# Products on ones, a 128-row spread of the norm weights and a fixed order in the opening of a two-layer trunk

## The chip, the core and the metric

The kernel runs on one core of one Trainium2 chip. The metric is the device time of one execution in microseconds (us), lower is better. Engines are TensorE (PE, its weight loads PEld), VectorE (DVE), ScalarE (ACT), GpSimd (POOL) and SyncE (SP), whose queue issues most loads.

## The reference

x has 512 tokens of 1024 features. Layer 0 has mixer A, layer 1 mixer B (latent attention); each layer ends with a squared-ReLU MLP. What matters here is the beginning of mixer A:

```python
h = rms_norm(x, attn_norm[0])
proj = h @ w_in                      # 1024 x 2120
q, k, v, qi, ki, wi = jnp.split(proj, cuts, axis=-1)
qi = partial_rope(qi.reshape(bsz, seq, IDX_HEADS, IDX_DIM), cos_i, sin_i, IDX_ROT)
ki = partial_rope(ki[:, :, None, :], cos_i, sin_i, IDX_ROT)[:, :, 0, :]
logits = jnp.einsum('bthd,bsd->bths', qib, ki)
score = jnp.einsum('bths,bth->bts', jax.nn.relu(logits), wib)
_, sel = lax.top_k(score, top_k)     # 128 of at most 512 keys for each token
```

Columns 1536 to 2120 of `w_in` (qi, ki, wi) feed the selection; the other 1536 columns are q, k and v.

## The kernel before

**Tiles.** Four token tiles of 128 rows, `xt[0..3]`. Tile 0 is special: its queries may see 128 keys at most, so no selection is needed, and only its 64 `ki` columns are computed. The order of the tiles is therefore 1, 2, 3, 0.

**Products in three passes.** Every float32 operand is split into a high and a low part. `mm3` makes three products for each pair: high x high (L227), high x low weight (L228), low activations x high weight (L229).

**Weights.** The class `Weights` holds one list of chunks for the whole program. `fetch` loads the next chunk on SP's queue into one of three raw buffers (L109). `convert` makes `w_hi` (mostly ScalarE, L143) and `w_lo` = raw - `w_hi` (GpSimd, or VectorE where the chunk says "v"; L150) in one of five pairs of buffers. `take` hands chunks to the consumer and converts some ahead. The columns 1536 to 1828 come in three chunks `w0`, `w1`, `w2` of 3, 3 and 2 blocks of 128 rows, the columns 1828 to 2120 in `w3`, `w4`, `w5`, the columns of k and v in `w6` and so on.

**Norm.** The row of norm weights is loaded into one partition (`g_row`), and two products with a row of ones (`one_row`, K = 1) spread it over 128 partitions in PSUM (`g_ps`, L316). `gains` multiplies a tile by it in two halves of 512 columns (`h`, VectorE, L477). `turn` transposes `h` with TensorE in two groups of four (`tps`, L454); ScalarE copies each group as `hT_hi` (L458), VectorE subtracts for `hT_lo` (L459). `factor` squares the tile (ScalarE, `junk`, L483), and a small VectorE operation (L484) and a GpSimd power (L485) make the factor 1/rms, which is applied when results leave PSUM (`out_of`, L715).

**The opening.** `idx_rows` multiplies tiles 1 to 3 with `w0` to `w2` (`ip`, 24 products of 292 columns for a tile); `rope_tables` makes the angles' sines and cosines on VectorE and ScalarE; `idx_tile` multiplies the four tiles with `w3` to `w5` (tile 0: 24 products of 64 columns). Then `proj_tiles` begins with the products of k and v (`pp`), among which the scores are computed. VectorE then runs the top-k selection beside the further projections.

**Order.** The tile framework orders the instructions of each engine by priorities and its own estimate of times. Only inside `with tc.manual_schedule(...)` does an engine keep the order of the code; before the change that holds for TensorE from `idx_tile` on. An engine works through its row strictly in order.

## Time and profile before

| | us |
|---|---|
| median of 3 runs (1151.34 to 1152.82) | 1151.39 |
| profiled execution | 1150.95 |
| its span, first to last instruction | 1149.2 |
| TensorE busy in the span | 1117.5 (97%) |
| VectorE / ScalarE / GpSimd busy | 754.8 / 619.7 / 670.0 |

Busy TensorE is the sum of overlapping, pipelined products, so 97% doesn't mean that it works at its peak. In a timeline a row gives start, length, engine, source line, output <- inputs and shape; the spacing of starts, not the length, is what a product costs in a dense row. Idle time in front of an instruction and what ended it stand in square brackets.

### The profile page before, as it was taken

How to read it: one execution, taken by the hardware profiler on the slowest of the kernel's cores; microseconds unless marked ns; L12 is line 12 of the kernel's file. 1: busy time of each engine (PE TensorE's matmuls, PEld its weight loads, DVE VectorE, ACT ScalarE, POOL GpSimd, SP SyncE). 2: the span in 40 equal slices, each digit the busy share in tenths (PEclk: the TensorE clock that was granted, in tenths of full speed). 3: DMA queues.
4: the chain of work that ended last, by engine and by line, in shares of the span. 5: the costliest groups of instructions: out<-in, count | busy, mean ns of one | idle time of the engine just before them, and what ended most of it. 6: DMA issues, size and time to landing. Idle time of an engine off the chain costs nothing.

```text
span 1149.2 us, 16018 instructions
## 1 busy us (share of the span) xinstructions
PE 1117.5 (97%) x5725; PEld 949.2 (83%) x5725; DVE 754.8 (66%) x1399; ACT 619.7 (54%) x1143; POOL 670.0 (58%) x508
## 2 busy tenths in 40 slices
PE   8999899989999999999999999899999999999997
PEld 7788788869888888888889898787988888888886
DVE  6699798673566466466566788676556466556664
ACT  6574896534544554454445776563564454464452
POOL 5498533543657857856702643554557756865772
PEclk9999999989999999999999999999999999999999
DMA  6413100242224314413322200111424313412402
GB/s 200 123 55 110 38 1 1 76 150 87 75 72 147 106 58 130 133 58 103 86 62 79 76 23 34 56 56 56 167 63 138 128 49 117 147 61 87 147 10 83
DMA packets 65465, 99.04 MB, mean 86 GB/s; under 512 B 3173, under 2 KB 41833, under 8 KB 65386
## 3 DMA queue, kind: packets, MB, share of 16 engines
q1 hardware_dynamic: 65386, 98.03, 26.9%
q8 instruction: 45, 0.74, 0.3%
q14 instruction: 34, 0.28, 0.1%
HBM read 95.92 MB, written 2.10 MB: 85 GB/s over the span
## 4 chain that ended last, share of the span: by engine, by line
PE 90%; DVE 3%; ACT 3%; issue 2%; POOL 1%; DMA 1%; SPq 0%; DVEq 0%; POOLq 0%; ACTq 0%
PE dn L1226 23%; PE up L227 10%; PE up L229 10%; PE up L228 10%; PE s_ps L560 3%; PE o_ps L622 3%; PE pt_ps L579 2%; PE wo_ps L227 2%; PE wo_ps L228 2%; PE wo_ps L229 2%; PE pp L227 2%; PE pp L229 2%; PE pp L228 2%; PE tps L454 1%; PE dn L228 1%
## 5 line engine op out<-in xcount | busy, mean ns | idle before, releaser
L148 POOL TENSOR_TENSOR w_lo<-quad,w_hi 128x512 fp32r<-128x512 f32 x196 | 274.7, 1433 | 163.1 <-ACT w_hi L143 155.7
L150 POOL TENSOR_TENSOR w_lo<-w_raw,w_hi 128x1024 fp32r<-128x1024 f32 (+4 forms) x117 | 264.4, 2278 | 86.7 <-ACT w_hi L143 71.6
L1229 DVE TENSOR_TENSOR x<-dn,x 128x512 f32<-128x512 f32 x196 | 134.9, 690 | 139.5 <-PE dn L1226 139.4
L228 PE MATMUL up<-hT_lo,w_hi 128*128 128x512 f32 (+1 forms) x576 | 210.8, 367 | 0.0
L227 PE MATMUL up<-hT_hi,w_hi 128*128 128x512 f32 (+1 forms) x576 | 210.3, 368 | 0.0
L229 PE MATMUL up<-hT_hi,w_lo 128*128 128x512 f32 (+1 forms) x576 | 208.8, 367 | 0.0
L143 ACT CAST w_hi<-w_raw 128x1024 fp32r<-128x1024 f32 (+6 forms) x112 | 111.7, 1006 | 141.1 <-PE dn L1226 62.2
L143 ACT CAST w_hi<-quad 128x1024 fp32r<-128x1024 f32 x98 | 101.2, 1050 | 100.0 <-DVE quad L86 71.7
L1226 PE MATMUL dn<-w_hi,lh 128*128 128x512 f32 x392 | 152.5, 389 | 0.0
L1226 PE MATMUL dn<-w_lo,lh 128*128 128x512 f32 x392 | 152.5, 389 | 0.0
L1226 PE MATMUL dn<-w_hi,ll 128*128 128x512 f32 x392 | 152.5, 389 | 0.0
L1191 DVE TENSOR_TENSOR ll<-u,lh 128x512 fp32r<-128x512 f32 x106 | 99.2, 966 | 40.7 <-ACT lh L1190 40.7
L229 PEld LDWEIGHTS up<-hT_hi,w_lo 128*128 128x128 f32 x576 | 109.1, 190 | 17.6
L227 PEld LDWEIGHTS up<-hT_hi,w_hi 128*128 128x128 f32 x576 | 109.0, 190 | 17.6 <-ACT hT_hi L458 0.2
L228 PEld LDWEIGHTS up<-hT_lo,w_hi 128*128 128x128 f32 x576 | 109.1, 190 | 17.4
L86 DVE TENSOR_TENSOR quad<-quad 128x1024 f32<-128x1024 f32 x56 | 68.4, 1221 | 65.3 <-POOL w_lo L148 65.3
L1190 ACT CAST lh<-u 128x512 fp32r<-128x512 f32 x106 | 62.9, 620 | 75.0 <-DVE u L1203 66.6
L1226 PEld LDWEIGHTS dn<-w_hi,ll 128*128 128x128 f32 x392 | 73.6, 188 | 15.3
L1226 PEld LDWEIGHTS dn<-w_hi,lh 128*128 128x128 f32 x392 | 73.6, 188 | 15.3
L1226 PEld LDWEIGHTS dn<-w_lo,lh 128*128 128x128 f32 x392 | 73.6, 188 | 15.3
L573 ACT ACTIVATE p<-p,m 128x128 f32<-128x128 f32 (+3 forms) x128 | 72.0, 564 | 16.3 <-DVE m L568 15.5
L592 ACT CAST pt_hi<-pt_ps 128x128 fp32r<-128x128 f32 (+3 forms) x128 | 53.0, 423 | 27.8 <-PE pt_ps L579 25.3
(237 smaller groups left out, 2249.8 us busy)
## 6 DMA issues: line engine op xcount, KB each, us to landing
w_raw<-in_mlp_w_up_dram SPq DMA_DIRECT2D x64, 512.0 KB, 3.7
quad<-in_mlp_w_down_dram SPq DMA_DIRECT2D x56, 512.0 KB, 3.6
w_raw<-in_a_w_in_dram SPq DMA_DIRECT2D x12, 512.0 KB, 3.6
w_raw<-in_a_w_out_dram SPq DMA_DIRECT2D x8, 512.0 KB, 3.2
w_raw<-in_mlp_w_down_dram SPq DMA_DIRECT2D x8, 512.0 KB, 4.5
w_raw<-in_b_w_out_dram SPq DMA_DIRECT2D x8, 512.0 KB, 3.7
x<-in_x_dram SPq DMA_DIRECT2D x4, 512.0 KB, 7.5
w_raw<-in_b_w_kv_up_dram SPq DMA_DIRECT2D x4, 512.0 KB, 3.9
```

The lines of the kernel that those rows point to most:

```text
L86: self.nc.vector.tensor_sub(q[o], q[l], q[r])
L143: nc.scalar.copy(h, v)
L148: nc.gpsimd.tensor_sub(l[:, cs], v[:, cs], h[:, cs].bitcast(F32))
L150: (nc.gpsimd if engs[1] == "p" else nc.vector).tensor_sub(l, v, h.bitcast(F32))
L227: nc.tensor.matmul(ps, lh, rh, start=first, stop=False)
L228: nc.tensor.matmul(ps, lh, rl, start=False, stop=False)
L229: nc.tensor.matmul(ps, ll, rh, start=False, stop=last)
L573: nc.scalar.activation(U["p"][:, :N], U["p"][:, :N], AF.Exp, bias=U["m"], scale=-1.0, accum_out=pair["sums"][:, c:c + 1])
L1190: nc.scalar.copy(lh, v)
L1191: nc.vector.tensor_sub(ll, v, lh.bitcast(F32))
L1226: nc.tensor.matmul(pp[t], l[:, k, ts], r[:, k, :], start=first and k == 0 and m == 0, stop=k == 1 and m == 2, skip_group_check=True)
L1229: last = nc.vector.tensor_add(x[:, cs], pp[t], x[:, cs])
```

## The change

1. Before any input has landed, seven products of a 128x128 tile of ones (kept in `xt[0]`) run on TensorE into the bank `rest`.
2. `g_row` becomes a tile of 128 rows of zeros, whose row 0 is loaded by ScalarE's queue; the spread uses the 128x128 matrix `first` (row 0 ones, others zero) in place of `one_row`.
3. The first chunk is split: `w0` has one block, `w1` two, `w2` three, `w3` two. So what was `w3` is now `w4`. Tile 1 is loaded in two halves, and the order on SP's queue is written out: tile 1, `w0`, `w1`, tile 2, `w2`, positions, tile 3, `w3`, tile 0.
4. The order of TensorE, ScalarE and VectorE in the opening is written by hand. The products of the fourth chunk with tile 1 stand ahead of the transposes of tile 0. `take(1, 4)` converts nothing ahead; `W.ahead(n)` does where it is called.
5. The square and the factor are separate (`squares`, `factor`); `rope_tables` stands behind the factor of tile 3.
6. `ang` and the first steps of `turns` are kept in PSUM instead of SBUF.

```diff
+    def ahead(self, n):
+        while len(self.done) < min(self.taken + n, len(self.items)):
+            self.convert()
...
-    W.rows(a_w_in[0][0:3 * P], 1536, 1828, 3, "av")
+    W.rows(a_w_in[0][0:P], 1536, 1828, 1)
+    W.rows(a_w_in[0][P:3 * P], 1536, 1828, 2, "av")
...
+    g_row = ht.tile([P, D], F32, name="g_row", tag="h", bufs=2)
+    first = const.tile([P, P], F32, name="first")
+    with tc.high_priority(2000):
+        nc.vector.memset(g_row[:, 0:512], 0.0)
+        nc.gpsimd.memset(g_row[:, 512:D], 0.0)
+        nc.scalar.dma_start(g_row[0:1], attn_norm[0:1])
+    nc.vector.memset(xt[0][:, 0:P], 1.0)
+    rest = bank("rest", 7)
+    for _ in range(7):
+        nc.tensor.matmul(rest[:, 0:P], xt[0][:, 0:P], xt[0][:, 0:P], start=True, stop=True)
+    nc.vector.memset(first, 0.0)
+    nc.vector.memset(first[0:1], 1.0)
...
-        nc.tensor.matmul(g_first[c], one_row, g_row[:, c * 512:(c + 1) * 512], start=True, stop=True)
+        nc.tensor.matmul(g_first[c], first, g_row[:, c * 512:(c + 1) * 512], start=True, stop=True)
...
-            ang = tp.tile([P, 2, NT, n], F32, name="ang")
+            both = bank("ang", 4)
+            ang, turns = (both[:, o:o + 2 * NT * n].rearrange("p (a t n) -> p a t n", a=2, t=NT) for o in (0, 256))
...
+                with tc.manual_schedule(engines={mybir.EngineType.PE, mybir.EngineType.Activation,
+                                                 mybir.EngineType.DVE}):
+                    nm.gains(1)
+                    w0, w1 = W.take(1, 4)[0], W.take(1, 4)[0]
+                    nm.turn(1)
+                    idx_rows(1, 0, w0)
+                    idx_rows(1, 1, w1)
+                    w2 = W.take(1, 4)[0]
+                    nm.gains(2)
+                    nm.turn(2)
+                    idx_rows(2, 0, w0)
+                    idx_rows(2, 1, w1)
+                    ps = token_positions(pr)
+                    w3 = W.take(1, 4)[0]
+                    nm.gains(3)
+                    idx_rows(1, 3, w2)
+                    nm.turn(3)
+                    nc.vector.tensor_copy(pos, ps[:, :NT])
+                    nm.squares(pr, 1)
+                    idx_rows(2, 3, w2)
+                    idx_rows(3, 0, w0)
+                    idx_rows(3, 1, w1)
+                    idx_rows(3, 3, w2)
+                    nm.gains(0)
+                    idx_rows(1, 6, w3)
+                    nm.turn(0)
+                    nm.squares(pr, 2)
+                    W.ahead(1)
+                    nm.squares(pr, 3)
+                    W.ahead(2)
+                    nm.factor(1)
+                    out_of(inat[1][:, :292], ips[1][:, :292], 1)
+                    nm.squares(pr, 0)
+                    W.ahead(3)
+                    idx_rows(2, 6, w3)
+                    nm.factor(2)
+                    idx_rows(3, 6, w3)
+                    nm.factor(3)
+                with tc.issue_after(nm.factored.ins):
+                    rope_tables()
```

Where the instructions stand now is shown at three places. Numbers behind names are buffer numbers; `tps` and `hT` of the rows belong to the tile that the text names.

ScalarE before, from the copy of tile 1's second half to the first of tile 3 (`tps_230`); `w3` and `w4` are the first two chunks of the columns 1828 to 2120.

```order
L458 CAST hT_hi_131<-tps_150 128x4x128
L143 CAST w2_hi_167<-w2_raw_97 128x584
L458 CAST hT_hi_131<-tps_185 128x4x128
L483 ACTIVATE junk_388,lead_71<-x0_84 128x1024
L143 CAST w3_hi_212<-w3_raw_100 128x876
L458 CAST hT_hi_131<-tps_192 128x4x128
L143 CAST w4_hi_361<-w4_raw_165 128x876
L458 CAST hT_hi_131<-tps_230 128x4x128
```

The changed kernel's ScalarE, from the chunk `w3` to the chunk `w5`; `tps_302` and `tps_309` are tile 0, `w4` is what `w3` was.

```order
L148 CAST w3_hi_231<-w3_raw_118 128x584
L482 CAST hT_hi_150<-tps_249 128x4x128
L482 CAST hT_hi_150<-tps_256 128x4x128
L505 ACTIVATE junk_264,lead_71<-x1_85 128x1024
L482 CAST hT_hi_150<-tps_302 128x4x128
L482 CAST hT_hi_150<-tps_309 128x4x128
L505 ACTIVATE junk_316,lead_71<-x2_86 128x1024
L148 CAST w4_hi_318<-w4_raw_121 128x876
L505 ACTIVATE junk_324,lead_71<-x3_87 128x1024
L148 CAST w5_hi_326<-w5_raw_199 128x876
```

The cast of that chunk moved from ahead of tile 3's copies to behind tile 0's copies and a square.

GpSimd before, from the second chunk's low half on.

```order
L150 TENSOR_TENSOR w1_lo_162<-w1_raw_94,w1_hi_161 128x876
L485 TENSOR_TENSOR lead_71<-lead_71,neghalf_69 128x1
L150 TENSOR_TENSOR w2_lo_168<-w2_raw_97,w2_hi_167 128x584
L485 TENSOR_TENSOR lead_71<-lead_71,neghalf_69 128x1 x2
L150 TENSOR_TENSOR w3_lo_213<-w3_raw_100,w3_hi_212 128x876
L150 TENSOR_TENSOR w4_lo_362<-w4_raw_165,w4_hi_361 128x876
```

GpSimd in the changed kernel; the rows on `lead` are the powers of the factors.

```order
L155 TENSOR_TENSOR w2_lo_196<-w2_raw_114,w2_hi_195 128x876
L155 TENSOR_TENSOR w3_lo_232<-w3_raw_118,w3_hi_231 128x584
L511 TENSOR_TENSOR lead_71<-lead_71,neghalf_69 128x1 x2
L155 TENSOR_TENSOR w4_lo_319<-w4_raw_121,w4_hi_318 128x876
L511 TENSOR_TENSOR lead_71<-lead_71,neghalf_69 128x1
L155 TENSOR_TENSOR w5_lo_327<-w5_raw_199,w5_hi_326 128x876
L511 TENSOR_TENSOR lead_71<-lead_71,neghalf_69 128x1
L155 TENSOR_TENSOR w6_lo_338<-w6_raw_235,w6_hi_337 128x584
```

Each of the low halves `w4`, `w5` and `w6` now has powers ahead of it, which wait for squares of ScalarE.

VectorE in the changed kernel, from tile 1's first gain half on; `h_161`, `h_201`, `h_237` are tiles 1, 2, 3.

```order
L501 TENSOR_TENSOR h_161<-x1_85,g_ps_124 128x512
L501 TENSOR_TENSOR h_161<-x1_85,g_ps_125 128x512
L155 TENSOR_TENSOR w1_lo_169<-w1_raw_111,w1_hi_168 128x584
L483 TENSOR_TENSOR hT_lo_151<-tps_172,hT_hi_150 128x4x128
L483 TENSOR_TENSOR hT_lo_151<-tps_179,hT_hi_150 128x4x128
L501 TENSOR_TENSOR h_201<-x2_86,g_ps_124 128x512
L501 TENSOR_TENSOR h_201<-x2_86,g_ps_125 128x512
L483 TENSOR_TENSOR hT_lo_151<-tps_204,hT_hi_150 128x4x128
L483 TENSOR_TENSOR hT_lo_151<-tps_211,hT_hi_150 128x4x128
L352 CAST posf_227<-posi_104 4x128
L501 TENSOR_TENSOR h_237<-x3_87,g_ps_124 128x512
```

VectorE in the kernel before, over the same work.

```order
L477 TENSOR_TENSOR h_182<-x2_86,g_ps_107 128x512
L484 TENSOR_SCALAR lead_71<-lead_71 128x1
L459 TENSOR_TENSOR hT_lo_132<-tps_143,hT_hi_131 128x4x128
L477 TENSOR_TENSOR h_227<-x3_87,g_ps_106 128x512
L477 TENSOR_TENSOR h_227<-x3_87,g_ps_107 128x512
L484 TENSOR_SCALAR lead_71<-lead_71 128x1
L459 TENSOR_TENSOR hT_lo_132<-tps_150,hT_hi_131 128x4x128
L340 CAST posf_320<-posi_102 4x128
```

The cast of the positions stood behind tile 3's gains and stands ahead of them now; the gains of tiles 2 and 3 stood ahead of `hT_lo` and stand behind it now.

## Rows read from the trace of the kernel before

**Rows 1.** The page, part 4: the chain that ended last, by engine.
```profile
PE 90%; DVE 3%; ACT 3%; issue 2%; POOL 1%; DMA 1%; SPq 0%; DVEq 0%; POOLq 0%; ACTq 0%
```

**Rows 2.** TensorE's waits over the span: total us, times, longest.
```profile
PE g_ps L316 <- DMA g_row<-in_attn_norm_dram: 4.3, 1, 4.3
```

**Rows 3.** Stages: length, busy us (count) by engine, granted clock, DMA share, GB/s.
```profile
60.00:117.00 57.00, 57.00 (x261) 46.76 (x261) 54.81 (x147) 33.06 (x62) 49.14 (x63) 1.00 0.28 85
...
130.00:180.00 50.00, 47.55 (x318) 41.12 (x316) 46.38 (x140) 45.02 (x132) 18.34 (x17) 1.00 0.00 1
```

**Rows 4.** Timeline of TensorE in the opening: start us, length us, what.
```profile
4.26 3.75 PE L316 MATMUL g_ps<-g_row,one_row 1*128 1x512 f32 x4 [4.26 <-DMA g_row<-in_attn_norm_dram]
...
10.72 0.61 PE L227 MATMUL ip<-w_hi,hT_hi 128*128 128x292 f32 x1 [0.52 <-ACT hT_hi L458]
...
14.06 0.45 PE L227 MATMUL ip<-w_hi,hT_hi 128*128 128x292 f32 x1
...
14.51 0.30 PE L229 MATMUL ip<-w_hi,hT_lo 128*128 128x292 f32 x1
14.64 0.29 PE L227 MATMUL ip<-w_hi,hT_hi 128*128 128x292 f32 x1
...
15.17 0.60 PE L454 MATMUL tps<-ident,h 128*128 128x128 f32 x4
15.53 0.38 PE L229 MATMUL ip<-w_hi,hT_lo 128*128 128x292 f32 x1
...
34.79 0.20 PE L227 MATMUL ip<-w_hi,hT_hi 128*128 128x64 f32 x1
...
37.39 0.48 PE L227 MATMUL pp<-w_hi,hT_hi 128*128 128x512 f32 x1
```

**Rows 5.** Timeline of SP's queue: the load of the norm weights.
```profile
1.17 0.33 SPq L306 DMA_DIRECT2D g_row<-in_attn_norm_dram  x1
```

**Rows 6.** Timeline of VectorE in the opening.
```profile
0.80 0.06 DVE L232 MEMSET ones<- 128x1 f32 x1 [0.80 <-PEq L1283]
...
6.34 0.69 DVE L477 TENSOR_TENSOR h<-x,g_ps 128x512 f32<-128x512 f32 x1 [0.55 <-PE g_ps L316]
7.36 1.07 DVE L150 TENSOR_TENSOR w_lo<-w_raw,w_hi 128x876 fp32r<-128x876 f32 x1 [0.33 <-ACT w_hi L143]
...
13.16 1.20 DVE L340 CAST posf<-posi 4x128 f32<-4x128 int32 x1
```

**Rows 7.** Timeline of ScalarE in the opening.
```profile
8.15 1.06 ACT L483 ACTIVATE junk<-x 128x1024 bf16<-128x1024 f32 x1 [0.82 <-DMA x<-in_x_dram]
...
9.26 0.92 ACT L143 CAST w_hi<-w_raw 128x876 fp32r<-128x876 f32 x1
10.09 0.58 ACT L458 CAST hT_hi<-tps 128x512 fp32r<-128x512 f32 x1
...
14.20 0.92 ACT L143 CAST w_hi<-w_raw 128x876 fp32r<-128x876 f32 x1
```

**Rows 8.** Timeline of GpSimd in the opening.
```profile
1.06 0.52 POOL L322 MEMSET smask<- 128x512 f32 x1
...
12.85 1.44 POOL L150 TENSOR_TENSOR w_lo<-w_raw,w_hi 128x584 fp32r<-128x584 f32 x1
14.24 0.55 POOL L485 TENSOR_TENSOR lead<-lead,neghalf 128x1 f32<-128x1 f32 x1
...
15.61 4.11 POOL L150 TENSOR_TENSOR w_lo<-w_raw,w_hi 128x876 fp32r<-128x876 f32 x2
```

**Rows 9.** The page, part 6: loads, KB each, median us from issue to landing.
```profile
x<-in_x_dram SPq DMA_DIRECT2D x4, 512.0 KB, 7.5
```

**Rows 10.** Stages of one us behind a gap of TensorE, columns as in rows 3.
```profile
250.00:251.00 1.00, 0.00 (x0) 0.00 (x0) 1.00 (x1) 0.58 (x1) 0.98 (x1) 0.50 1.06 377
...
256.00:257.00 1.00, 1.00 (x7) 1.00 (x7) 1.00 (x3) 0.00 (x0) 0.00 (x0) 0.60 1.04 385
```

**Rows 11.** Timeline of TensorE at the end of that gap.
```profile
251.68 1.94 PE L454 MATMUL tps<-ident,h 128*128 128x128 f32 x8 [3.74 <-DVE h L426]
```

More of the change, by code (lines that the diff above doesn't have):

```diff
@@ L326, in trunk, with token_positions @@
     ropeC, ropeS = {}, {}
+    pos = const.tile([P, NT], F32, name="pos")
+    def token_positions(tp):
+        posf = tp.tile([NT, P], F32, name="posf")
+        nc.vector.tensor_copy(posf, posi)
+        ps = bank("pos_ps", 4)
+        nc.tensor.transpose(ps[:, :NT], posf, ident[:NT, :NT])
+        return ps
     def rope_tables():
@@ L743, in mixer_a @@
-                idx_rows(3, 0, w0)
-                idx_rows(2, 3, w1)
-                idx_rows(3, 3, w1)
-                nm.gains(0)
-                nm.turn(0)
-                rope_tables()
-                nm.factor(pr, 3)
-                w2 = W.take(1, 2)[0]
-                for t in range(1, NT):
-                    idx_rows(t, 6, w2)
+                with tc.manual_schedule(engines={mybir.EngineType.PE, mybir.EngineType.Activation,
[36 more added lines that the diff above has]
+                    nm.factor(3)
```

56 lines of the change are left out of this document (20 added, 36 removed).

## The prediction

> **What bounds the kernel now.** I read the chain of work that ended last first: 90% of the span is TensorE [rows 1]. So the question of the change is when TensorE gets its work. Then TensorE's waits: the largest of the whole run is the first one, 4.3 us until the norm weights have landed [rows 2]. The stage table shows that nothing absorbs a shift behind the opening: from 60 to 117 us TensorE is busy for 57.00 of 57 us, VectorE for 54.81 with the top-k selection that itself waits for TensorE's scores [rows 3]. A shift of the first `pp` product therefore reaches the end whole.
>
> The timeline of TensorE gives the opening [rows 4]. Norm weights are spread from 4.26, the first `ip` product starts at 10.72, and from there on there is no idle time up to the first `pp` product at 37.39. At 14.06 a 292-column product lasts 0.45, from 14.51 on 0.30, and then they start 0.13 apart: between the two the engine goes from the lower of its two clock levels (1.2 GHz) to the higher (2.4 GHz), though the granted-clock column shows 1.00 throughout. The scheduler kept TensorE fed by mixing tiles and chunks freely. The changed kernel fixes the order of TensorE, ScalarE and VectorE by hand, so I walk its order with the durations of these rows, up to the first `pp` product.
>
> **Prices.** TensorE: product of 292 columns 0.134 at the higher clock, of 64 columns 0.11 (24 from 34.79 to 37.39), four transposes 0.36 until the next start and 0.60 until they can be read, spreading 1024 columns 3.75 at the lower clock [rows 4]. VectorE: a gain half 0.69, a `hT_lo` of the same shape the same, about 0.6 from start to start; a 584-column `w_lo` 0.71, as 584/876 of 1.07 [rows 6]. ScalarE: `hT_hi` 0.58 (0.5 to the next start), a square 1.1 to the next start, a 876-column `w_hi` 0.92 [rows 7]. GpSimd: `w_lo` of 876 columns 2.05, of 584 columns 1.44, a power 0.55 (0.5 to the next start) [rows 8]. A hand-over costs 0.05, as from `hT_hi` (10.09 + 0.58) to the product at 10.72.
>
> **Part 1, products on ones.** They need the memset of `x0`, behind a new 512-column memset on VectorE, which begins at 0.80 [rows 6]; no such memset on VectorE is in the trace, GpSimd's took 0.52 [rows 8]. So they start at about 1.6. Seven of 128x128 cost 7/8 of 3.75 = 3.3 at the lower clock, up to 4.9. Only the spread itself and the load of `x0` wait for them. The norm weights now leave ScalarE's queue after two memsets, at about 1.4 instead of 1.17 [rows 5], so I put their landing at 4.5: hidden under the products on ones. The ends are 4.2 and 4.9; neither is late.
>
> **Part 2, spread from 128 rows.** It starts at 4.9, 0.6 later than before, and is worth its place only if the clock has risen. Before, the rise came 3.7 us after the first 292-column product; the 3.75 us of spreading from one row had not brought it [rows 4]. In another place the engine sat idle for 3.74 us, went on at 251.68, and the granted clock was back only in the slice of 256, 5.1 us later [rows 10, 11]. Counted from 1.6 that is 5.3 to 6.7; I take 6.0. The first half is then 59% done at 6.0 and ends at 6.4, the second at 7.3. Transposes, then `hT_hi`: first `ip` product at 7.35 + 0.60 + 0.05 + 0.58 + 0.05 = 8.65, against 10.72. The Trainium skill (TensorE: Matmul & The Clock Gate, Part 1) says that the moment of the rise differs from run to run of one kernel, which one trace can't show; if so, a rise already at 4.9 or only behind the spread moves the sum by -0.55 to +1.7; by the rows it is 8.65.
>
> **Part 3, the fixed order up to the last token tile.** TensorE's row has 60 products before the transposes of tile 0: 24 of tile 1 (all of its first 292 columns), 18 each of tiles 2 and 3. Until the ninth product of tile 2 it hangs on VectorE: after the second gain half (8.05) come `w1_lo`, two `hT_lo` and two gain halves in a row, so tile 2 can be turned at 10.6 and 11.2, its `hT_hi` is there at 11.8, its `hT_lo` at 12.5, and the nine end at 13.5 instead of 11.8: 1.7 us idle. Then VectorE casts `posi` before it makes the gains of tile 3. This cast of 4x128 took 1.20 before, and ended when GpSimd's 584-column `w_lo`, which started at 12.85, had ended [rows 6, 8]. In the new order `w3_lo`, again 584 columns, starts at about 13.05, when the cast comes up at 13.1. If held: the gains of tile 3 start 1.3 later; if it slips in first: nothing. I take held, as in the row. The Trainium skill (SBUF — State Buffer, Terms) says that VectorE and GpSimd lock their shared port for a whole instruction and that the loser blocks; by it the cast loses the 1.3 us, by bandwidth sharing it would lose about 0.2, and the forecast would be 1.1 lower.
>
> From 13.5: 1.3 held, 0.2 for the position transpose, 9 products 1.2, tile 3's two groups of transposes 0.72, 0.15 for the change of tile, 33 products 4.4. Tile 0 is turned at 21.5 (20.2 if not held). The loads set none of this. On the load queue `x0` stands behind the load of `w3`, which now waits for `w0_lo` (about 6.4), and took 7.5 from issue to landing before [rows 9]: about 14.5, needed near 19. Tile 2's gains come at 9.9, later than the 8.15 until which ScalarE waited for its load [rows 7]. The halved first tile, the small first chunk and its low half on GpSimd (0.72, as 292/584 of 1.44) are all done before 8.65; uncovered, the last would cost its 0.72.
>
> **Part 4, where the fourth and later chunks are converted.** This is the largest term. Before, the first chunk of the second 292 columns (`w3` there) had its cast at 14.20 and its low half from 15.61, long before tile 0 was turned [rows 7, 8]. Now ScalarE's row puts the cast of `w4` (the same weights) behind both copies of tile 0 and the square of tile 2, and GpSimd's row puts `w4_lo` behind two powers that hang on that square. From the start of tile 0's transposes: 0.60 + 0.05, copies 0.5 + 0.5, square 1.1, cast 0.92, low half 2.05, hand-overs 0.1 = 5.8 us. TensorE has only 0.72 of transposes and 12 products (1.6) plus one high product in that time: it idles 3.4. Next, `w5_lo` follows after a power: 0.5 + 2.05 = 2.55 against nine products (1.2), 1.3 idle; `w6_lo`: 0.5 + 1.44 = 1.95 against 1.2, 0.75 idle. Sum 5.4 us of idle time that the kernel before does not have. After the first low product of `w6`: five products 0.67, tiles 2 and 3 48 x 0.134 = 6.43, tile 0 2.6.
>
> 21.5 + 5.8 + 2.55 + 1.95 + 9.7 = 41.5 for the first `pp` product, against 37.39: **4.1 us later**.
>
> **Part 5, the rest.** Angles in PSUM: the table chain stands behind the factors now, and is needed by the first `rope_v`, after the second 292 columns of tile 1; at about 33 it has been over for some microseconds. Nothing on the path, so zero; without this cover a held table copy would cost up to one `w_lo`, 2.05. The scheduler also orders the attention between 120 and 180 anew; there TensorE idles 2.45 us in 130 to 180 [rows 3], so at most that is to be won, and I take as much to be lost: value 0, bounds -2.4 and +2.4.
>
> **The sum.** The profiled execution took 1150.95 us for a span of 1149.2, 0.4 under the median of 1151.39. 1150.95 + 4.1 = 1155.05, on the median's scale 1155.5.
>
> **Rivals.**
> *Short stalls.* The clock is up at 4.9 (first product 8.1: -0.55), the cast slips in (-1.3), half of the 1.7 on VectorE vanishes (-0.85): 4.1 - 2.7 = 1.4 later, 1152.8. For it: the cast's race is decided by 0.05 us. Against it: the 5.4 of part 4 stays.
> *Faster, the head start wins.* If the low halves of `w4` to `w6` are written before TensorE asks for them, TensorE runs on densely from 8.65: of the 26.67 us from 10.72 to 37.39, the first 3.8 up to 14.51 hold 11 products and four transposes, 1.8 at the higher clock; without these 2.0 the first `pp` product is at 33.3, 4.1 earlier: 1147.3. It decides when `w4_lo` ends less than 2.5 us after tile 0's first transpose; the rows make that 5.8, and only an earlier place of the cast than the order shows would change it.
> *The clock falls in the new gap.* At 250 it was granted 0.50 after 3.74 us without work and stayed so until 256.8 [rows 10, 11]. The new gap is of 3.4. A fall in it costs little while GpSimd sets the pace, but half of whatever is left of some 6.8 us once it doesn't: 0.8 to 3.4 on top, 1156.3 to 1158.9. The Trainium skill (TensorE: Matmul & The Clock Gate, HAM oscillation) says that waits between bursts put the clock back.
> *The ones don't raise the clock.* Spread until 8.65, first product at 10.35: 1.7 on top, 1157.2.
>
> **Chances.** The forecast (1153.8 to 1156.3) 0.45, clock falls 0.17, ones without effect 0.08, short stalls 0.21, faster 0.09. Less than 0.2% either way (1149.1 to 1153.7) is what a measurement of this kernel can't tell from no change. Slower: 0.45 + 0.17 + 0.08 = 0.70; same 0.21; faster 0.09. The range runs from 1151.8, inside the short stalls, to 1159.0: it leaves out the faster case, a corner of the short stalls and the sum of both clock rivals.
>
> **What would show it.** In the new profile: products on ones from about 1.6; first `ip` product at 8 to 9; tile 0's transposes at 20 to 22; then TensorE waiting for GpSimd's `w_lo` three times, 3.4, 1.3 and 0.75; first `pp` product at 40 to 42. A first `pp` product before 37.4 makes the forecast wrong; so does a `w4_lo` that ends before tile 0 is turned. If `pp` comes late and the time doesn't, the loss was given back between 117 and 180.

## The result and the profile after

| | before | after |
|---|---|---|
| median of the runs taken side by side, us | 1152.34 | 1159.27 |
| lowest and highest, us | 1149.77, 1153.19 | 1155.34, 1160.47 |
| profiled execution: time, span, us | 1150.95, 1149.2 | 1160.47, 1158.5 |
| its mean granted clock | 0.993 | 0.986 |

The ratio is 1.0055, with a 95% interval of 1.0043 to 1.0066. On the scale of the prediction (1151.39) that is 1157.7 us, 1156.3 to 1159.0: slower, as forecast, 2.2 us above the forecast of 1155.5 and inside its range. The place is where the "clock falls" rival had put it.

The chain that ended last is TensorE again, with GpSimd at 3% in place of 1% [rows 1]:

```profile
PE 86%; DVE 4%; issue 4%; ACT 3%; POOL 3%; POOLq 0%; DVEq 0%; ACTq 0%
```

TensorE's waits up to 60 us (total, times, longest). The 4.3 us for the norm weights [rows 2] are gone; the conversions of weights have come in their place:

```profile
PE ip L233 <- POOL w_lo L155: 2.4, 2, 1.8
PE rest L319 <- DVE x L316: 1.6, 1, 1.6
PE ip L232 <- ACT w_hi L148: 1.0, 1, 1.0
```

TensorE's timeline (start, length; in brackets the idle time before and what ended it), to be held against [rows 4]:

```profile
1.60 3.36 PE L319 MATMUL rest<-x 128*128 128x128 f32 x14 [1.60 <-DVE x L316]
4.75 3.27 PE L337 MATMUL g_ps<-g_row,first 128*128 128x512 f32 x4
7.86 0.60 PE L478 MATMUL tps<-ident,h 128*128 128x128 f32 x4
...
9.21 0.38 PE L232 MATMUL ip<-w_hi,hT_hi 128*128 128x292 f32 x1
...
25.08 0.40 PE L232 MATMUL ip<-w_hi,hT_hi 128*128 128x292 f32 x1 [0.98 <-ACT w_hi L148]
27.27 0.40 PE L233 MATMUL ip<-w_lo,hT_hi 128*128 128x292 f32 x1 [1.79 <-POOL w_lo L155]
...
28.05 0.45 PE L232 MATMUL ip<-w_hi,hT_hi 128*128 128x292 f32 x1
...
29.80 0.61 PE L233 MATMUL ip<-w_lo,hT_hi 128*128 128x292 f32 x1 [0.58 <-POOL w_lo L155]
...
43.06 0.47 PE L232 MATMUL pp<-w_hi,hT_hi 128*128 128x512 f32 x1
```

The first `ip` product comes 1.5 us earlier than before, the first `pp` product 5.7 us later. GpSimd's rows show what the second and third wait hang on, three low halves with a power between each two:

```profile
25.18 2.04 POOL L155 TENSOR_TENSOR w_lo<-w_raw,w_hi 128x876 fp32r<-128x876 f32 x1
27.18 0.55 POOL L511 TENSOR_TENSOR lead<-lead,neghalf 128x1 f32<-128x1 f32 x1
27.69 2.06 POOL L155 TENSOR_TENSOR w_lo<-w_raw,w_hi 128x876 fp32r<-128x876 f32 x1
...
30.23 1.44 POOL L155 TENSOR_TENSOR w_lo<-w_raw,w_hi 128x584 fp32r<-128x584 f32 x1
```

Stages of one us (columns as in rows 3; the granted clock is the third number from the end). TensorE hardly works from 24 to 27, and from 28 to 34.8 its clock is at the lower level, 0.50:

```profile
24.00:25.00 1.00, 0.10 (x1) 0.00 (x0) 0.21 (x2) 1.00 (x4) 0.86 (x2) 1.00 0.00 0
25.00:26.00 1.00, 0.40 (x1) 0.19 (x1) 0.00 (x0) 1.00 (x4) 1.00 (x2) 1.00 0.00 0
26.00:27.00 1.00, 0.00 (x0) 0.00 (x0) 0.82 (x4) 1.00 (x3) 1.00 (x1) 1.00 0.00 0
...
28.00:29.00 1.00, 1.00 (x6) 0.87 (x4) 0.88 (x4) 1.00 (x3) 1.00 (x1) 0.51 0.63 78
...
34.00:35.00 1.00, 1.00 (x7) 1.00 (x6) 1.00 (x3) 0.77 (x2) 0.98 (x2) 0.57 0.81 309
...
65.70:122.70 57.00, 57.00 (x261) 46.75 (x260) 54.81 (x147) 33.03 (x62) 49.15 (x63) 1.00 0.27 85
```

The last line is the stage of [rows 3], 5.7 us later and otherwise the same to 0.03 us: nothing absorbs the shift. What fixes its beginning are the transposes of the index keys (`kip`), from which the selection starts: 42.60 before, 48.30 after, and 74.5 us later the first `s_ps` product in both (117.13 and 122.82). So I use the keys' transposes as the marker below. Their rows, before and after:

```profile
42.60 0.60 PE L814 MATMUL kip<-ident,inat 128*64 128x128 f32 x4
```

```profile
48.30 0.60 PE L859 MATMUL kip<-ident,inat 128*64 128x128 f32 x4
```

Of the profiled 9.3 us, 3.6 lie behind that marker: 0.6 by the end of the first attention and the start of the MLP, 0.85 in the first MLP, 1.4 in the second attention, 0.45 in the last MLP, 0.3 in small pieces. The largest of these is again the clock. Around 755 it is granted at 0.50 for 6.8 us where before it was 3.4 us:

```profile
755.00:756.00 1.00, 0.58 (x3) 0.59 (x3) 0.94 (x2) 0.36 (x1) 1.00 (x2) 0.53 0.00 0
...
761.00:762.00 1.00, 1.00 (x8) 0.98 (x7) 0.08 (x1) 0.79 (x3) 0.92 (x2) 0.55 0.75 176
```

The same stages of the kernel before, where the lower clock starts and ends:

```profile
748.00:749.00 1.00, 0.84 (x4) 0.84 (x5) 0.77 (x2) 0.10 (x1) 1.00 (x1) 0.66 0.00 0
...
751.00:752.00 1.00, 1.00 (x7) 1.00 (x6) 0.85 (x3) 0.49 (x2) 1.00 (x1) 0.63 0.88 135
```

Lengths like these differ between executions of one kernel: the profiled execution is the slowest of the changed kernel's ten, with a mean granted clock of 0.986, and the quickest took 1155.34 us at 0.993. `angles_sbuf` below has TensorE's order of the changed kernel behind the opening, no stretch at the lower clock near 755, and needs 767.9 us from the keys to the last `wo_ps` product of the second attention, against 770.4 in the changed kernel and 767.5 before. So I don't count them to the change. The opening's 5.7 us are nearly all of the 6.3 us that the ratio gives.

### The profile page after: what moved, and what is told of

Same layout as the page of the kernel before. It is cut to its first block, busy times and chain, and to the rows that moved or that the text cites. A ratio compares the mean times of both kernels' runs of the same rounds, so it can differ in the third digit from the quotient of the medians.

```text
span 1158.5 us, 16063 instructions
## 1 busy us (share of the span) xinstructions
PE 1125.7 (97%) x5739; PEld 955.7 (82%) x5739; DVE 761.8 (66%) x1402; ACT 618.5 (53%) x1144; POOL 673.1 (58%) x510
## 4 chain that ended last, share of the span: by engine, by line
PE 86%; DVE 4%; issue 4%; ACT 3%; POOL 3%; POOLq 0%; DVEq 0%; ACTq 0%
PE dn L1271 22%; PE up L232 9%; PE up L233 9%; PE up L234 9%; PE o_ps L648 3%; PE s_ps L586 3%; PE pt_ps L605 2%; PE wo_ps L232 2%; PE wo_ps L233 2%; PE wo_ps L234 2%; PE pp L232 2%; PE pp L234 2%; PE pp L233 2%; POOL w_lo L153 2%; PE tps L478 1%
## 5 line engine op out<-in xcount | busy, mean ns | idle before, releaser
L155 POOL TENSOR_TENSOR w_lo<-w_raw,w_hi 128x1024 fp32r<-128x1024 f32 (+5 forms) x118 | 266.9, 2281 | 92.1 <-ACT w_hi L148 89.0
L148 ACT CAST w_hi<-w_raw 128x1024 fp32r<-128x1024 f32 (+7 forms) x113 | 112.0, 998 | 153.3 <-PE dn L1271 55.3
L1236 DVE TENSOR_TENSOR ll<-u,lh 128x512 fp32r<-128x512 f32 x106 | 95.1, 927 | 42.6 <-ACT lh L1235 42.6
```

The source lines that it names most:

```text
L148: nc.scalar.copy(h, v)
L155: (nc.gpsimd if engs[1] == "p" else nc.vector).tensor_sub(l, v, h.bitcast(F32))
L1236: nc.vector.tensor_sub(ll, v, lh.bitcast(F32))
```

## The experiments

The theory after the result: TensorE waits for the conversions of `w4` to `w6` (part 4 of the prediction), and the clock that falls in that wait adds to it. Rivals: the loss lies behind the opening; other parts of the change (ones, spread, loads, angles) make it; VectorE, held by GpSimd, sets the keys whatever TensorE does. A table of all kernels, each from the trace of one execution (us; "turned" is the start of the transposes of tile 0 and of the index keys; the last column is the ratio to the kernel before, from all executions, with its interval):

| kernel | first `ip` | tile 0 turned | first `pp` | keys turned | ratio |
|---|---|---|---|---|---|
| before | 10.72 | 21.89 | 37.39 | 42.60 | 1 |
| after | 9.21 | 21.46 | 43.06 | 48.30 | 1.0055 (1.0043 to 1.0066) |
| early_chunks | 8.55 | 20.67 | 35.35 | 40.59 | 1.0023 (1.0011 to 1.0035) |
| gap_filled | 8.38 | 20.49 | 41.81 | 48.78 | 1.0079 (1.0064 to 1.0094) |
| gap_13 | 8.93 | 21.16 | 41.20 | 46.42 | 1.0031 (1.0015 to 1.0047) |
| no_ones | 9.40 | 21.35 | 43.45 | 48.69 | 1.0045 (1.0030 to 1.0059) |
| no_ones_one_row | 9.64 | 23.25 | 44.94 | 50.18 | 1.0102 (1.0083 to 1.0121) |
| before_ones | 10.85 | 22.75 | 38.26 | 43.48 | 1.0006 (0.9992 to 1.0020) |
| opening_alone | 11.41 | 24.26 | 39.78 | 46.75 | 1.0053 (1.0036 to 1.0071) |
| free_order | 11.58 | 23.69 | 39.23 | 44.46 | 1.0021 (1.0008 to 1.0034) |
| angles_sbuf | 7.96 | 20.08 | 43.53 | 50.50 | 1.0073 (1.0054 to 1.0093) |
| chunks_behind_copies | 8.56 | 20.67 | 37.19 | 44.23 | 1.0018 (1.0004 to 1.0032) |
| behind_copies_psum | 8.33 | 20.44 | 36.96 | 42.19 | 0.9993 (0.9985 to 1.0002) |
| early_two_ones | 9.56 | 21.49 | 36.17 | 41.40 | 0.9983 (0.9974 to 0.9992) |

**The conversions moved ahead (early_chunks).**

```diff
                     nm.squares(pr, 1)
                     idx_rows(2, 3, w2)
+                    W.ahead(1)
                     idx_rows(3, 0, w0)
+                    W.ahead(2)
                     idx_rows(3, 1, w1)
+                    W.ahead(3)
...
                     nm.squares(pr, 2)
-                    W.ahead(1)
                     nm.squares(pr, 3)
-                    W.ahead(2)
...
                     nm.squares(pr, 0)
-                    W.ahead(3)
```

> The changed kernel with one thing moved: the conversions of the weight chunks w4, w5 and w6 stand ahead of the transposes of tile 0 (behind the square of tile 1, as soon as TensorE has let go of the buffers of w0 and w1), instead of behind tile 0's copies and the squares. Theory 1, the conversion chain of part 4 and the clock that falls while TensorE waits for it are the loss: no wait for w_lo is left after tile 0's transposes, which start at 21.5 as in the changed kernel; 0.79 of transposes, 12 + 72 products of 0.134 and 2.6 for tile 0 put the first pp product at 36.1 to 36.6 instead of 43.06, the granted clock stays 1.00 from 24 to 36, and the time falls by 6.5 to 7 us, to 0.5 us above to 1.5 us below the kernel before. Rival, the loss is only partly in the opening (3.6 us of the profiled 9.3 come behind the first pp product): the first pp product at 36.1 to 36.6, but the time stays 2 to 4 us above the kernel before.

No wait of TensorE for a low half is left up to 60 us:

```profile
35.35 0.47 PE L232 MATMUL pp<-w_hi,hT_hi 128*128 128x512 f32 x1
```

The first `pp` product starts at 35.35, 7.7 us earlier than in the changed kernel (0.8 of that is an earlier tile 0), and the keys 2.0 us earlier than before the change. So the conversions and what follows from them are the whole loss of the opening. But the time stays 2.6 us above the kernel before, as the rival had it: 4.6 us are lost further on. TensorE's waits from 780 to 825, in this kernel and in the one before:

```profile
PE wo_ps L232 <- DVE x L557: 2.4, 3, 0.8
```

```profile
PE wo_ps L227 <- DVE x L531: 0.3, 1, 0.3
```

There the scheduler had set the last output products of the second attention in another order. The edit doesn't touch that place; that its model of the times carried the new opening there is my reading, which no run shows by itself. From the last `o_ps` to the last `wo_ps` product it is 29.3 us in the three kernels with that order (early_chunks, opening_alone, no_ones_one_row) and 25.3 to 25.4 in the eleven others. Part of that is only work that has moved to the other side of the last `o_ps` product: from the keys to the last `wo_ps` product early_chunks needs 770.3 us, and no_ones and gap_13, with as long at the lower clock, need 766.5 and 766.8. Some 3.5 us are its price here; the same comparison gives 2.4 to 3 for opening_alone and no_ones_one_row.

**The clock in the gap (gap_filled, gap_13).**

```diff
                     idx_rows(3, 6, w3)
+                    keep = bank("keep", 0)
+                    for _ in range(28):
+                        nc.tensor.matmul(keep[:, 0:P], ident, ident, start=True, stop=True)
                     nm.factor(3)
```

> The changed kernel with 28 products of 128x128 on the identity matrix put into TensorE's row where it waits for w4, after the last product of w3; their result is used by nobody. They last 28 x 0.107 = 3.0 us at the higher clock and end at about 27.0, before w4_lo ends at 27.2, so by themselves they cost nothing. Theory 1, the clock that falls in the gap adds to the conversion chain: the granted clock stays 1.00 from 24 to 35, the products behind w6_lo (31.7) take 9.7 us and not 11.4, and the first pp product starts at 41.3 to 41.7 instead of 43.06: 1.4 to 1.7 us off the time of the changed kernel. Rival, GpSimd's chain alone sets the pace: first pp product and time within 0.4 us of the changed kernel. Second rival, the later waits for w5 and w6 (1.3 and 0.75) bring the clock down all the same: 0.5 or less is won.

My size was wrong: 28 products are 56 rows in the trace and lasted 0.224 each, to 29.3, so they delayed the first `w4` products by themselves. The clock stayed at 1.00 and the first `pp` product came at 41.81, but the keys at 48.78: they now waited 1.6 us for VectorE. With 13:

> The changed kernel with 13 products of 128x128 on the identity matrix in TensorE's gap ahead of w4 (28 were too many: each took 0.224, so they ended at 29.3, behind w4_lo). 13 x 0.224 = 2.9 us, from about 23 to 26, before w4_lo ends at 26.2 to 27.2. The order of all work behind the opening is that of the kernel before, as in no_ones. Theory 1, the clock stays up and TensorE is only held by GpSimd's chain: first pp product 9.7 behind the end of w6_lo, at 40.4 to 41.4 instead of 43.06. Theory 2, VectorE's rotation of tile 0's key, held by GpSimd's low halves, then sets the key transposes, as in gap_filled (48.8 there with the first pp product at 41.8): key transposes at 46.5 to 48.5, and 1 us or less is won against the 48.3 of the changed kernel. If the transposes come 5.2 behind the first pp product (45.6 to 46.6), 1.7 to 2.7 us are won at that point and VectorE is not in the way.

The two stages that had the lower clock in the changed kernel:

```profile
28.00:29.00 1.00, 0.46 (x4) 0.22 (x2) 0.87 (x4) 1.00 (x4) 1.00 (x1) 1.00 0.67 145
...
34.00:35.00 1.00, 1.00 (x9) 1.00 (x8) 1.00 (x4) 0.49 (x2) 0.96 (x2) 1.00 0.59 225
```

From the end of `w6_lo` (31.38) to the first `pp` product it is now 9.8 us, as the prediction had it, where the changed kernel needed 11.4 (31.67 to 43.06). The clock is worth 1.6 us there. The keys came 5.2 behind, so VectorE was not in the way this time, and the time fell to 3.6 us above the kernel before.

**The ones and the 128-row tile (no_ones, no_ones_one_row, before_ones).**

```diff
-    nc.vector.memset(xt[0][:, 0:P], 1.0)
-    rest = bank("rest", 7)
-    for _ in range(7):
-        nc.tensor.matmul(rest[:, 0:P], xt[0][:, 0:P], xt[0][:, 0:P], start=True, stop=True)
```

> The changed kernel without the seven products on ones (and without the memset that feeds them). The spread of the norm weights is then TensorE's first work, at 4.2 to 4.7. Theory 1, the ones bring the higher clock earlier: the spread takes 3.75 at the lower clock and ends at 8.0 to 8.5 against 8.02, but the 292-column products stay 0.24 apart until 10.5 to 14.5, so the first pp product starts 0.5 to 2.0 us later than 43.06 and the time grows by as much. Rival, the ones have no effect that counts (VectorE's gains and low halves set the pace up to 14 us): first pp product and time within 0.3 us of the changed kernel.

The keys came 0.4 us later, the time is 1.2 us lower with overlapping intervals: nearer the rival. And TensorE was not at the lower clock up to 10.5, as I had expected: the transposes went from 0.21 to 0.11 apart at 8.5, 0.6 behind the end of the spread. The next kernel changes one line of it:

```diff
-        nc.tensor.matmul(g_first[c], first, g_row[:, c * 512:(c + 1) * 512], start=True, stop=True)
+        nc.tensor.matmul(g_first[c], first[0:1], g_row[0:1, c * 512:(c + 1) * 512], start=True, stop=True)
```

> The kernel no_ones (the changed kernel without products on ones) with one thing changed: the norm weights are spread from one row, as in the kernel before, instead of from 128 rows of which 127 are zero. The order of all engines in the opening is that of no_ones; the scheduler orders the end of the second attention as in early_chunks and opening_alone. In no_ones the four products of the spread took 3.75 us at the lower clock, and the products behind them ran at the higher one (0.13 apart from 9.4 on). Theory 1, products on one row do not bring the higher clock and products on 128 rows do: the spread takes 3.75 again, the first ip product comes at 10.0 to 10.8 instead of 9.40, products are 0.24 apart up to 14 to 16, and the key transposes come 0.5 to 2.5 us later than the 48.69 of no_ones. Rival, the clock rises some microseconds behind TensorE's first work whatever it works on: first ip product at 9.4, key transposes within 0.3 of 48.69. For the order at the end of the second attention: from the last o_ps to the last wo_ps product 29.3 us instead of 25.4 by theory 1 of chunks_behind_copies, so that the time is 4 to 6.5 us above no_ones; 25.4 if that order costs nothing.

TensorE's timeline of no_ones, and behind it that of no_ones_one_row:

```profile
4.16 3.75 PE L333 MATMUL g_ps<-g_row,first 128*128 128x512 f32 x4 [4.16 <-DMA g_row<-in_attn_norm_dram]
...
10.36 0.29 PE L232 MATMUL ip<-w_hi,hT_hi 128*128 128x292 f32 x1
10.49 0.29 PE L233 MATMUL ip<-w_lo,hT_hi 128*128 128x292 f32 x1
```

```profile
4.17 3.75 PE L333 MATMUL g_ps<-g_row,first 1*128 1x512 f32 x4 [4.17 <-DMA g_row<-in_attn_norm_dram]
...
10.77 0.45 PE L232 MATMUL ip<-w_hi,hT_hi 128*128 128x292 f32 x1
11.02 0.45 PE L233 MATMUL ip<-w_lo,hT_hi 128*128 128x292 f32 x1
...
14.09 0.29 PE L233 MATMUL ip<-w_lo,hT_hi 128*128 128x292 f32 x1
```

The same columns for the same 3.75 us, from 128 rows or from one: behind the first, products run at 2.4 GHz, behind the second they last 0.45 until 12.4 and the keys come 1.5 us later. The first `ip` product, at 9.64, came between the two theories, since the eight transposes lasted 1.97 and not 1.65. Of the 1.5 us, 0.7 are a wait for the `posi` cast, which is held here (see below). For the order at the end of the second attention the 29.3 us came as expected; the time is 6.6 us above no_ones, in which the keys, that order and longer stretches at the lower clock come together (20.5 us instead of 10.2 from the keys to the last `wo_ps` product).

```diff
+    nc.vector.memset(xt[0][:, 0:P], 1.0)
+    rest = bank("rest", 7)
+    for _ in range(4):
+        nc.tensor.matmul(rest[:, 0:P], xt[0][:, 0:P], xt[0][:, 0:P], start=True, stop=True)
     for t in (1, 2, 3, 0):
```

> The kernel before with four products on ones put ahead of the spread of the norm weights, and nothing else: no engine's order changes anywhere, the norm weights are spread from one row as before. Four products end at 1.6 + 4 x 0.43 = 3.3, before the norm weights land at 4.2, so they delay nothing. Theory 1, work on ones brings the higher clock earlier: 6 us after 1.6, at 7.5 to 8, instead of 14.5; the transposes of tile 1 stand 0.11 instead of 0.21 apart, no product of 292 columns lasts 0.45, and the first pp product comes 0.5 to 2 us earlier than 37.39, the time 0.5 to 2 us lower. Rival, the products on ones change neither the clock nor the first pp product: same time within 0.5 us.

Theory 1 fell. Products on ones in front of a spread from one row did not bring the clock: 292-column products lasted 0.45 up to 15.9, longer than before, and the keys came 0.9 us later.

**Parts of the change apart (opening_alone, free_order).** opening_alone is the kernel before with the ones, the 128-row tile and its load on ScalarE's queue; free_order is the changed kernel with

```diff
-                with tc.manual_schedule(engines={mybir.EngineType.PE, mybir.EngineType.Activation,
-                                                 mybir.EngineType.DVE}):
+                with ExitStack():
```

> The kernel before with the opening of the changed one alone: seven products on ones, the norm weights on ScalarE's queue into a 128-row tile, the spread from it. Loads, chunks, order of the engines and the angles are as before. The spread ends at 8.0, as in both kernels. Theory 1, the earlier clock is worth its microseconds if the order is not fixed: transposes 0.11 apart instead of 0.21, first ip product at 10.0 to 10.4 instead of 10.72, no half-clock products up to 14.5, so the first pp product comes 1 to 2.5 us earlier than 37.39 and the time is 1 to 2.5 us below the kernel before. Rival, the head start is taken up by a wait for inputs, low halves or w_lo: first pp product and time within 0.4 us of the kernel before.

> The changed kernel with the fixed order of TensorE, ScalarE and VectorE taken away from the first projection: the scheduler orders these engines, all else is as in the changed kernel. In its order the casts of w4, w5 and w6 stand on ScalarE where their loads and buffers allow, the squares lie in between, and the transposes of the tiles are spread among products. Theory 1, the fixed order with its late conversions is the loss: no wait of more than 1 us for w_lo behind tile 0's transposes, first pp product at 35.5 to 38.5, the time 3 to 6 us below the changed kernel and within 2 us of the kernel before. Rival, the other parts of the change (loads, small first chunk, squares apart) hold TensorE as long: first pp product later than 40, time less than 2 us below the changed kernel.

In opening_alone the spread began at 5.78, after a wait of 0.8 for a factor on VectorE. The clock was up 0.5 us behind it, 4.5 us earlier than in the kernel before: the eight transposes from 9.33 on lasted 1.65, as in no_ones. Then TensorE waited 1.5 us for the copy of the positions, and within that wait the clock fell again, until 16.8:

```profile
13.00:13.50 0.50, 0.00 (x0) 0.00 (x0) 0.50 (x3) 0.50 (x3) 0.50 (x2) 0.89 0.77 243
...
16.50:17.00 0.50, 0.50 (x4) 0.50 (x4) 0.50 (x2) 0.00 (x0) 0.50 (x2) 0.70 0.00 0
```

It waited 1.6 us more for the keys' rotation, and the end of the second attention has the 29.3 us. Neither theory expected a loss of 4.2 us at the keys; what the early clock is worth without these waits, this run doesn't show.

free_order did what theory 1 said of the wait: none for a low half is left, the keys are 3.8 us earlier and the time is 3.9 us less than in the changed kernel. But the first `pp` product (39.23) came later than the 38.5 expected, and the time stays 2.4 us above the kernel before, not within 2; its first `ip` product was the latest of all (11.58) and its clock was low for 6.8 us from 10.7 on. So the fixed order with its late conversions makes 3.8 of the 5.7 us, and the rest of the change gains nothing when the scheduler orders it: the keys are 1.9 us later than before.

**Angles back in SBUF (angles_sbuf).**

```diff
-            both = bank("ang", 4)
-            ang, turns = (both[:, o:o + 2 * NT * n].rearrange("p (a t n) -> p a t n", a=2, t=NT) for o in (0, 256))
+            ang = tp.tile([P, 2, NT, n], F32, name="ang")
+            turns = tp.tile([P, 2, NT, n], F32, name="turns0")
```

> The changed kernel with the angles and the turns back in SBUF, and nothing else; the order of all engines but VectorE's own operand places is that of the changed kernel. Theory 1, the angles in PSUM are worth nothing, since the table chain lies beside other work: first pp product 42 to 43.1, the same time within 1 us. Rival, the chain's operations on SBUF are held by GpSimd's low halves of 2.05 us, of which three run from 25 to 31.7 at the same time: up to three of its 18 operations last 2 us longer, the tables come 2 to 6 us later than 37.3, and with them the rotations and the key transposes: up to 5 us slower.

The rival, by another way than I had named; the intervals of its time and the changed kernel's overlap. One operation of the chain is held by `w5_lo`; its row in angles_sbuf, then in the changed kernel:

```profile
26.34 2.11 DVE L378 TENSOR_SCALAR turns<-ang 128x96 f32<-128x96 f32 x1
```

```profile
27.31 0.27 DVE L378 TENSOR_SCALAR ang<-ang 128x96 f32<-128x96 f32 x1
```

The factor of tile 0 stands behind part of the chain on VectorE, its power ahead of `w6_lo` on GpSimd, and GpSimd idled:

```profile
30.22 0.66 POOL L511 TENSOR_TENSOR lead<-lead,neghalf 128x1 f32<-128x1 f32 x1 [1.84 <-DVE lead L510]
```

Without the held operation the factor would have been in time. The scheduler also set that factor three operations (0.8 us) later in the chain than in the changed kernel, so the hold alone is not all of the 1.84. From the end of `w4_lo` to the end of `w6_lo` it took 6.4 us instead of 4.45, from tile 0 to the first `pp` product 23.5 instead of 21.6 (the clock, low for 10.2 us there, has its part in that). Another 1.7 us went at the keys, where VectorE's rotation was held as in gap_filled. In the fixed order the angles in PSUM are worth about 2 us, this other place of the factor included.

**What the opening is worth without its late conversions (chunks_behind_copies, behind_copies_psum, early_two_ones).** In chunks_behind_copies `W.ahead(1)` stands ahead of `idx_rows(3, 0, w0)`, and `W.ahead(2)` and `W.ahead(3)` right behind `nm.turn(0)`.

> The changed kernel with w4 converted ahead of tile 0's transposes and w5 and w6 right behind tile 0's copies, ahead of the squares of tiles 2 and 3. Unlike in the kernel early_chunks the order of all work behind the opening is here the one of the kernel before, on every engine. Opening, by the rows: tile 0 turned at 20.5 to 21.5, w5_lo ends 4.6 later and TensorE waits 0.85 for it, a power stands ahead of w6_lo, which ends 6.5 after the turn (wait 0.75), then 9.7: first pp product at 36.7 to 37.7, the key transposes at 41.9 to 42.9 (42.60 in the kernel before). Theory 1, what early_chunks lost behind its opening (its keys were turned 2.0 us earlier than before, its time was 2.5 us above) comes from the other order at the end of the second attention (28.6 to 29.3 us from the last o_ps product to the last wo_ps product there, 25.3 in the kernel before): without that order the time is that of the kernel before plus the shift of the key transposes, -0.7 to +0.3 us. Rival, the lost microseconds hang on the changed opening itself: still 2 to 4 us above the kernel before.

The first `pp` product came at 37.19, as expected, the end of the second attention took 25.4 us, and the time is 2.1 us above the kernel before: the keys were the miss, 1.3 us later than the latest expected. The 2.1 us lie in the rival's range, but the keys alone, 1.6 us later than before, make most of them; the next run decides. VectorE's three operations on tile 0's key beside GpSimd's low halves:

```profile
39.38 2.36 DVE L415 TENSOR_TENSOR rope_v<-inat,ropeS_a 128x16 f32<-128x16 f32 x1
41.67 0.16 DVE L417 TENSOR_TENSOR rope_u<-inat,ropeC_a 128x16 f32<-128x16 f32 x1
41.86 2.22 DVE L418 TENSOR_TENSOR inat<-rope_u,rope_v 128x16 f32<-128x16 f32 x1
```

behind_copies_psum takes that rotation from TensorE's result:

```diff
-                            rope(nc.vector, att, "a", t, inat[t][:, 512:528], 1, HD)
...
+                            v = ps[:, 256:272]
+                            nc.vector.scalar_tensor_tensor(v.rearrange("p (b c) -> p b c", b=2), swapped, nm.y[0],
+                                                           Sn.rearrange("p (b c) -> p b c", b=2),
+                                                           op0=OP.mult, op1=OP.mult)
+                            nc.vector.scalar_tensor_tensor(u, ps[:, 0:16], nm.y[0], C, op0=OP.mult, op1=OP.mult)
+                            nc.vector.tensor_add(inat[t][:, 512:528], v, u)
```

> The kernel chunks_behind_copies (first pp product at 37.19, but the key transposes waited 1.7 us for VectorE's rotation of tile 0's key, whose three operations of 128x16 took 2.36, 0.16 and 2.22 beside GpSimd's low halves of 2.4) with that rotation read from PSUM: the two products of the rotation take TensorE's result in PSUM, times the factor, instead of its copy in SBUF, so each of the three operations has an operand in PSUM. Order behind the opening as in the kernel before. Theory 1, VectorE's operations are held by a low half on GpSimd only where all their operands lie in SBUF (in the changed kernel the 17 operations of the table chain on PSUM lasted 0.27 to 0.38 each beside three low halves, with the angles in SBUF one lasted 2.11): the three last 0.2 to 0.4, the key transposes come 5.2 behind the first pp product, at 42 to 43 instead of 44.2, and the time falls by 1.2 to 1.8 us against chunks_behind_copies, to the kernel before -0.5 to +0.7 us. Rival, an operation is held whatever its operands are: key transposes at 43.5 to 45, time as in chunks_behind_copies.

```profile
39.16 0.23 DVE L842 SCALAR_TENSOR_TENSOR ip<-ip,lead,ropeS_a 128x16 f32<-128x16 f32 x1
39.42 0.23 DVE L845 SCALAR_TENSOR_TENSOR rope_u<-ip,lead,ropeC_a 128x16 f32<-128x16 f32 x1
39.69 0.17 DVE L846 TENSOR_TENSOR inat<-ip,rope_u 128x16 f32<-128x16 f32 x1
```

Theory 1: keys at 42.19, 5.2 behind the first `pp` product, and 2.9 us less than chunks_behind_copies, of which the keys explain 2.0. The Trainium skill (SBUF — State Buffer, Who interferes with whom) says that VectorE shares a port pair with GpSimd only where both its inputs lie in SBUF or where it runs in a faster two-port mode, and that who comes first keeps the pair; these rows agree, 0.17 to 0.23 with one input in PSUM against 2.22 to 2.36. early_two_ones is early_chunks with that rotation and

```diff
-    for _ in range(7):
+    for _ in range(2):
```

> The kernel early_chunks (w4, w5 and w6 converted ahead of tile 0's transposes) with two products on ones instead of seven and the rotation of tile 0's key read from PSUM as in behind_copies_psum. With two products the scheduler leaves the order at the end of the second attention as in the kernel before; in the first attention, from 120 to 180, some products stand in another order. Opening, as in early_chunks: no wait for w_lo behind tile 0's transposes, first pp product at 35.3 to 36.5, key transposes at 40.5 to 41.8 (42.60 in the kernel before). Theory 1, the changed opening is worth 1 to 2 us once its conversions come early and nothing later is worsened: from the last o_ps to the last wo_ps product of the second attention 25.3 us again, and the time 0.5 to 2 us below the kernel before. Rival, the other order of the first attention costs what the opening wins (in gap_filled, with the same order there, the way from the key transposes to the first up product was 1.9 us longer): the time within 1 us of the kernel before.

Its waits up to 60 us, all but the first start:

```profile
PE g_ps L337 <- DMA g_row<-in_attn_norm_dram: 1.5, 1, 1.5
PE lp L909 <- DVE ki L873: 0.9, 1, 0.9
PE ip L234 <- DVE hT_lo L483: 0.4, 2, 0.2
```

The keys come at 41.40, the second attention's end takes 25.4 us, and the time is 0.9983 of the kernel before: 2.0 us below it (0.9 to 3.0), and faster than both kernels. From the keys to the first `up` product it took 211.6 us, 210.8 before, but with 8.8 us at the lower clock instead of 6.9; gap_13 and behind_copies_psum, in the order of the kernel before and with 8.7 and 9.0, needed 211.6 and 211.2. So no price of the other order of the first attention shows.

## Why the prediction was right, step by step

**Part 1, ones.** They ran from 1.60 to 4.75 (1.6 to 4.9 forecast), and the spread followed without a wait. Right; the times show no gain by them (1.0045 without, 1.0055 with).

**Part 2, the clock and the spread.** First `ip` product 9.21 instead of 8.65. The failing step is the moment of the rise: taken at 6.0 within 5.3 to 6.7, it fell in the last product of the spread, which began at 7.31; the three before it started 0.85 apart. Six other kernels with the same seven ones and the same spread had their first `ip` product between 7.96 and 8.93, so the moment differs between profiles with the same work up to there. The Trainium skill (TensorE: Matmul & The Clock Gate, Part 1), cited there, says it of runs of one kernel. The cause that I gave was wrong too. I counted the rise from the first of the ones; no_ones has none and the higher clock all the same, and one row in place of 128 takes it away. [Rows 4] had the hint, since 3.75 us of spreading had not raised it there, and I read it as a matter of time alone. Between no_ones and the changed kernel the ones move the keys by 0.4 us; but the changed kernel's profile has the latest rise of the seven, and the other six turned tile 0 at 20.08 to 21.16, 0.2 to 1.3 us ahead of no_ones (21.35).

**Part 3, up to tile 0.** Tile 0 was turned at 21.46 (21.5 forecast), by two errors that cancelled. The ninth product of tile 2 ended at 14.6 instead of 13.5, half of that inherited from the first `ip` product. The cast of `posi` was not held, which gave 1.3 back. Its row and that of `w3_lo` in the changed kernel, then in no_ones_one_row:

```profile
14.04 0.20 DVE L352 CAST posf<-posi 4x128 f32<-4x128 int32 x1
```

```profile
14.05 1.50 POOL L155 TENSOR_TENSOR w_lo<-w_raw,w_hi 128x584 fp32r<-128x584 f32 x1 [1.02 <-ACT w_hi L148]
```

```profile
15.04 1.42 DVE L348 CAST posf<-posi 4x128 f32<-4x128 int32 x1
```

```profile
14.94 1.44 POOL L155 TENSOR_TENSOR w_lo<-w_raw,w_hi 128x584 fp32r<-128x584 f32 x1 [1.55 <-ACT w_hi L148]
```

Who starts first, by 0.01 or 0.10 us, runs undisturbed. I had named the race, with a margin of 0.05, and took the wrong side.

**Part 4, the conversions.** The term that carried the forecast, right to 0.04 us: `w4_lo` ended 5.76 us after tile 0 was turned (5.8 forecast), `w5_lo` 2.53 later (2.55), `w6_lo` 1.92 later (1.95). early_chunks shows that this is the loss of the opening. The idle time was 3.4 us and not 5.4, because TensorE worked through the rest of it at the lower clock.

**The step that was mis-sized** is the 9.7 us from there to the first `pp` product: 11.4. I left the clock's fall to a rival with a chance of 0.17 and a price of 0.8 to 3.4 us; it happened, for 1.6 us, and gap_13 without it gives back the 9.8. It put the first `pp` product at 43.06 instead of 41.5. The price of the rival was right, its chance was too low: the clock fell in all four kernels that have this gap unfilled (also in no_ones, no_ones_one_row and angles_sbuf). The gap came out with 3.3 us between two low products. I had held my 3.4 against the 3.74 of [rows 11] and read these wrongly: [rows 10] have the clock at 0.50 from 250.0 on, 1.7 us before TensorE went on at 251.68, so it had fallen 2.1 us after the last product at the latest; in opening_alone it fell within a wait of 1.5.

**Part 5.** For the angles I put zero, because the table chain would lie beside other work. It does, but a factor stands behind it and `w6_lo` behind that factor's power. In SBUF the chain cost some 2 us there, part of them by the other place of that factor; PSUM saved them. For the attention's new order, zero within 2.4 either way: the changed kernel and angles_sbuf, with one order, needed 2.9 and 0.4 us more than the kernel before from the keys to the last `wo_ps` product, with other stretches at the lower clock. The nearest to a price: no_ones, gap_13 and behind_copies_psum, in the order of the kernel before and as long at the lower clock as angles_sbuf (10.2 us), needed 1.1 to 1.6 us less than it there, one profile each.

**The bound.** That a shift of the first `pp` product reaches the end whole was right where the keys followed it by 5.2 us. In gap_filled, opening_alone, angles_sbuf and chunks_behind_copies they came 7.0 behind, held on VectorE, a second path that I had not priced.

## What to carry to other kernels

When an order is fixed by hand, list for each load its cast, its low half and its first reader, with the engine each stands on: here three engines were ordered well for the start, and the fourth, GpSimd, ended the low half `w4_lo` some 3 us after TensorE had finished with the chunk before it. A short VectorE operation next to long GpSimd ones should read one input from PSUM, or, as in the rows above, it lasts as long as they do when it starts second. And where a scheduler orders the rest, compare its order of the whole program before calling a time the price of an edit: three kernels here lost about 3 us some 700 us behind the line that was changed.

## What the runs showed of the hardware that I had not expected

The four products of the spread last 3.75 us from one row and from 128 at the lower clock; behind the second the clock was up 0.6 us after the last of them (no_ones), behind the first 5, 6 and 8 us after (no_ones_one_row, the kernel before, before_ones). In all eleven profiles with the 128-row spread it was up by 10.0 us, in the three with one row not before 12.4. The rise in the seven profiles with seven ones in the fixed order fell between the first and the last product of the spread, 4.8 to 7.5 us into the span. VectorE's operations of 8 to 144 columns, 0.15 to 0.31 us by themselves, lasted up to 2.5 us behind a low half that had begun, while 512-column ones with an operand in PSUM kept their 0.69.
